# Two short down groups become one of four row blocks, and the plain last pair is finished token block by token block

## The chip, the core and the metric

The kernel runs on one core of a Trainium2 chip. The metric is the device time of one execution in microseconds. The core has a matrix engine (TensorE, PE in the profile; PEld is its loading of stationary operands), VectorE (DVE), ScalarE (ACT), GpSimd (POOL) and a queue for transfers (SyncE, SP). Matrix products are written to PSUM, which has eight banks; one bank holds 128 x 512 f32 values here. VectorE and ScalarE read the banks, and a bank can be written anew only when its reader is done.

## What is computed

One decoder layer over 512 tokens of width 1024. The part that the change touches is the feed-forward network (FFN), which stands at the beginning and near the end of the layer:

```python
def swiglu(x, w_gate, w_up, w_down):
    return (jax.nn.silu(x @ w_gate) * (x @ w_up)) @ w_down
...
    h = h + 0.5 * swiglu(rmsnorm(h, ffn1_norm[i]), ffn1_w_gate[i], ffn1_w_up[i], ffn1_w_down[i])
    n = rmsnorm(h, mix_norm[i]); z = n @ W_in          # attention and gated linear attention follow
    h = h + concat(attn_o, gla_o) @ w_out[i]
    h = h + 0.5 * swiglu(rmsnorm(h, ffn2_norm[i]), ffn2_w_gate[i], ffn2_w_up[i], ffn2_w_down[i])
    h = h + sigmoid(rmsnorm(h, ple_gate_norm[i]) @ ple_w_gate[i]) * emb
```

The inner width is 2816, that is 22 row blocks of 128. All of it is f32.

## The kernel before

Each f32 operand is held as the sum of two fp32r tiles, a rounded one (`hi`, made by ScalarE, line 130 for weights) and the remainder (`lo`, made by VectorE, line 131). A product of two operands is three matmuls into the same bank: hi x hi, hi x lo, lo x hi (`mm3`, line 172).

An FFN (`ffn`) walks over the 22 row blocks in 11 pairs; `fa` is the first block of a pair. For a pair it computes the gate projection (`gemm(0, ...)`, tiles `pg`, 48 matmuls of 512 columns) and the up projection (`gemm(1, ...)`, tiles `pu`, 48 matmuls), each in two banks of the tag `psT`. `factors` then applies silu, multiplies, and writes the result split in `acts_hi` and `acts_lo`. These have two slots, chosen by `j = (fa // 2) % 2`, so that two pairs are held at a time.

The down projection (`pd`) is not a plain product. `products(f0, f1)` takes a group of row blocks and uses seven products of sums and differences in the place of eight (a Strassen-Winograd scheme over halves of tokens, of columns and of even and odd row blocks). `ORDER` lists the products; for each the weights are one tile from the ring, and there are two token blocks `b`. A group of four row blocks needs 7 x 2 x 2 x 3 = 84 matmuls, one of two row blocks 42. Each product ends with two evictions by VectorE: into `U` (line 329, for products 1 and 6) or with `half_add` into the token tiles `h` (line 308, for the others). Products 2, 3 and 4 are added onto the banks of products 1, 5 and 7 after their first reading. Banks come from the tags `psA` (products 1 and 7) and `psG` (products 5 and 6), two banks each. At the end of an FFN `U` is added into three quarters of `h`, six instructions of line 308.

The last pair, row blocks 20 and 21, is multiplied plainly: for each column half `c0` and each of the four token blocks `t` six matmuls into a bank of `psA`, then a `half_add`. With the second column half a token block is complete and `done(t)` starts the next layer's normalization of it (two squares on ScalarE, a power on POOL, `nrm` on VectorE, line 261), and the transposes of block t - 1 (`ntr`, line 268, banks of `psG`), whose results are cast and subtracted once more. Behind the first FFN stands the mixing layer, which begins with `kvr`; behind the second the gate of the embeddings, `pgt`.

The groups before are (0, 4), (4, 8), (8, 12), (12, 16), (16, 18) and (18, 20). The first five run between gate and up projection of the pair that follows them; the sixth runs behind the loop, as does the plain pair:

```python
                if fa + 2 < NF and groups[0][1] == fa:
                    products(*groups.pop(0))
                gemm(1, 0, 512)
            factors(fa, pss)
        products(*groups.pop(0))
```

Weights come by transfers of SP's queue into raw tiles, are split, and lie in a ring of five `hi` and five `lo` tiles, with two more for the FFN's weights. `W.get(key)` splits up to four units ahead of the one that it is asked for, in the order in which `add_ffn` lists them. A ring tile comes free when its last matmul is done. A down group's weights are loaded as two transfers, even and odd row blocks.

The order of the instructions on each engine is laid down when the program is built: a scheduler takes them by program order as soon as their operands and banks are free in a timeline that it keeps (`schedule_with_timeline_sim=True`). So matmuls of the up projection fill places in which a product of the group isn't ready, and the queue of an engine isn't the order of the text.

Of the kernel before, what the change touches and what calls it, by code (L numbers as in the profile page):

```python
# [8 lines left out]
F32 = mybir.dt.float32  # L9
# [8 lines left out]
NT = S // P  # L18
# [3 lines left out]
NF = F // P  # L22
# [1 line left out]
NEG = -3.0e38  # L24
LEVELS = (64, 32, 16, 8, 4, 2, 1)

GROUPS = ((0, 4), (4, 8), (8, 12), (12, 16), (16, 18), (18, 20))

ORDER = ((1, 0), (5, 1), (2, 2), (3, 6), (7, 5), (6, 4), (4, 3))

# [110 lines left out]
def hymba_kernel(tc, A, out):  # L141
    nc = tc.nc
# [11 lines left out]
    def psA(name):  # L154
        return psp.tile([P, 512], F32, name=name, tag="psA", bufs=2)
# [16 lines left out]
    def mm3(o, l, r, start, stop_, **kw):  # L172

        mm(o, l[0], r[0], start, False, **kw)
        mm(o, l[0], r[1], False, False, **kw)
        mm(o, l[1], r[0], False, stop_, **kw)
# [14 lines left out]
    h = [hp.tile([P, D], F32, name=f"h{t}") for t in range(NT)]  # L191
    W = Weights(nc, rawp, ringp, 4)


    def add_ffn(i):
        g, u, d = A[f"ffn{i}_w_gate"], A[f"ffn{i}_w_up"], A[f"ffn{i}_w_down"]
        groups = [x for x in GROUPS]
        for f in range(0, NF, 2):
            W.add_cols(f"g{i}", g, f * P, 2)
            if f + 2 < NF and groups and groups[0][1] == f:  # L200
                W.add_products(f"d{i}", d, *groups.pop(0))
            W.add_cols(f"u{i}", u, f * P, 2)
        W.add_products(f"d{i}", d, *groups.pop(0))
        for c0 in (0, 512):
            W.add_rows(f"d{i}", d, NF - 2, 2, c0, 512)

# [71 lines left out]
    def tokens(t):  # L278
        return slice(t * P, (t + 1) * P)
# [10 lines left out]
    def ffn(i, nT, p, done, hi_p, raw_p, raw_tag, n_extra, rest=None):  # L290
        U = [p.tile([P, 512], F32, name=f"U{i}_{b}") for b in range(2)]
        acts_hi = hi_p.tile([P, 2, 7, 256], F32R, name=f"ahi{i}", tag="nlo")
# [14 lines left out]
        def half_add(hs, x):  # L307
            nc.vector.scalar_tensor_tensor(hs, x, 0.5, hs, ALU.mult, ALU.add)  # L308
# [29 lines left out]

        def factors(fa, pss):

            plain = fa == NF - 2
            j = (fa // 2) % 2
            cb = p.tile([P, 7, 256], F32, name=f"cb{i}_{fa}", tag="cb", bufs=1)
            for q in range(2):
                pg, pu = pss[q]
                sg = p.tile([P, S], F32, name=f"sg{i}_{fa + q}", tag="sg", bufs=2)
                nc.scalar.activation(sg, pg, AF.Silu)
                nc.vector.tensor_mul(cb[:, 2 * q:2 * q + 2, :].rearrange("p a c -> p (a c)"), pu, sg)  # L348
            n = 4 if plain else 7
            if not plain:  # L350
                nc.vector.tensor_sub(cb[:, 5, :], cb[:, 1, :], cb[:, 0, :])
                nc.vector.tensor_add(cb[:, 1, :], cb[:, 1, :], cb[:, 3, :])
                nc.vector.tensor_sub(cb[:, 4, :], cb[:, 1, :], cb[:, 0, :])
                nc.vector.tensor_sub(cb[:, 6, :], cb[:, 2, :], cb[:, 4, :])
            nc.scalar.copy(acts_hi[:, j, :n], cb[:, :n])
            nc.vector.tensor_sub(acts_lo[:, j, :n], cb[:, :n], acts_hi[:, j, :n].bitcast(F32))

        groups = list(GROUPS)
        for fa in range(0, NF, 2):
            pss = [(psT(f"pg{i}_{fa + q}"), psT(f"pu{i}_{fa + q}")) for q in range(2)]  # L360

            def gemm(m, a, b):
                for q in range(2):
                    wh, wl = W.get((f"{'gu'[m]}{i}", fa + q))
                    for k in range(KC):
                        mm3(pss[q][m][:, a:b], (wh[:, k, :], wl[:, k, :]),
                            (nT[0][:, k, a:b], nT[1][:, k, a:b]), k == 0, k == KC - 1)

            if fa == 0:
                gemm(0, 0, 256)  # L370
                gemm(1, 0, 256)
                if rest:
                    rest()
                gemm(0, 256, 512)
                gemm(1, 256, 512)
            else:
                gemm(0, 0, 512)
                if fa + 2 < NF and groups[0][1] == fa:
                    products(*groups.pop(0))
                gemm(1, 0, 512)  # L380
            factors(fa, pss)
        products(*groups.pop(0))
        for b in range(2):
            half_add(h[b][:, r], U[b])
            half_add(h[2 + b][:, l], U[b])
            half_add(h[2 + b][:, r], U[b])
        for c0 in (0, 512):
            wh, wl = W.get((f"d{i}", c0, NF - 2))
            for t in range(NT):
                ps = psA(f"pd{i}_{c0}_{t}")  # L390
                for q in range(2):
                    a = (1, 2 * q + t // 2, tokens(t % 2)) if ((NF - 2) // 2) % 2 else (0, 2 * q + t // 2, tokens(t % 2))
                    mm3(ps, tuple(x[:, a[0], a[1], a[2]] for x in (acts_hi, acts_lo)), (wh[:, q, :], wl[:, q, :]),
                        q == 0, q == 1)
                half_add(h[t][:, c0:c0 + 512], ps)
                if c0:
                    done(t)
        W.extra = None


# [590 lines left out]
```

## Time and profile before

| what | value |
|---|---|
| median of 3 runs | 1037.27 us (1036.75 to 1039.93) |
| the profiled execution's own time | 1041.27 us |
| its span, first to last instruction | 1039.5 us |
| mean granted TensorE clock | 0.986 |
| TensorE busy | 1006.9 us, 97% |
| VectorE busy | 673.4 us, 65% |
| ScalarE busy | 398.1 us, 38% |
| chain that ended last | 87% TensorE, 5% VectorE, 3% transfers |

The profile is of one execution. Matmuls are pipelined, and their ends are modelled, so that a busy TensorE isn't necessarily one at its peak: starts that follow each other are the better measure of its pace. The granted clock is a share of 2.4 GHz; 0.5 is the lower level, 1.2 GHz. A wait is put down to the semaphore that came last.

### The profile page before, as it was taken

What the parts mean: (1) busy time and instruction counts of PE and PEld (TensorE: products, weight loads), DVE (VectorE), ACT (ScalarE), POOL (GpSimd) and SP (SyncE); (2) the same over time, 40 slices, a digit from 0 to 9 for tenths busy, and PEclk for the clock granted to TensorE, in tenths of its full rate; (3) what the DMA queues carried; (4) which work ended last, traced back from release to release, by engine and by line L of the source; (5) the groups of instructions that cost most, each with busy time, mean ns of one, the idle gap of its engine ahead of it and who ended that gap; (6) DMA issues with size and microseconds to landing.
All of it is one profiled execution on the core that took longest, in us unless ns stands there. A gap on an engine that the chain in (4) does not pass through costs nothing.

```text
span 1039.5 us, 12500 instructions
## 1 busy us (share of the span) xinstructions
PE 1006.9 (97%) x5090; PEld 823.6 (79%) x5090; DVE 673.4 (65%) x904; ACT 398.1 (38%) x585; POOL 47.0 (5%) x58
## 2 busy tenths in 40 slices
PE   6999999999999979999999999999999999999798
PEld 5988888888888858877667789888888888887577
DVE  6486756666667586568875454767576666685853
ACT  6344333333323335554474243343323333233331
POOL 2300000000000001100000100000000000000100
PEclk9899999999999999999999799999999999999999
DMA  6843325042212053131103315242250523120521
GB/s 242 275 173 123 120 75 169 0 162 82 100 63 82 1 185 102 41 122 26 57 22 81 122 54 208 83 158 84 81 162 1 167 76 122 41 82 8 186 80 52
DMA packets 73148, 105.79 MB, mean 102 GB/s; under 512 B 5745, under 2 KB 55170, under 8 KB 73090
## 3 DMA queue, kind: packets, MB, share of 16 engines
q1 hardware_dynamic: 70786, 96.60, 28.4%
q0 software_dynamic: 2304, 8.39, 2.1%
q8 instruction: 40, 0.66, 0.3%
q14 instruction: 18, 0.15, 0.0%
HBM read 98.69 MB, written 6.29 MB: 101 GB/s over the span
## 4 chain that ended last, share of the span: by engine, by line
PE 87%; DVE 5%; DMA 3%; issue 2%; ACT 1%; POOL 1%; SPq 0%; ACTq 0%; POOLq 0%; DVEq 0%
PE pu L170 23%; PE pg L170 23%; PE pd L170 17%; PE pgt L170 4%; PE wo L170 3%; PE gv L170 2%; PE aq L170 2%; PE gqk L170 2%; DVE wlo L131 2%; PE gog L170 2%; DVE h L308 2%; PE gr L170 1%; PE sc L170 1%; PE pv L170 1%; PE kvr L170 1%
## 5 line engine op out<-in xcount | busy, mean ns | idle before, releaser
L130 ACT CAST whi<-wraw 128x1024 fp32r<-128x1024 f32 (+1 forms) x130 | 134.0, 1040 | 196.6 <-PE pd L170 123.6
L131 DVE TENSOR_TENSOR wlo<-wraw,whi 128x1024 fp32r<-128x1024 f32 (+1 forms) x126 | 151.5, 1206 | 59.5 <-ACT whi L130 56.6
L170 PE MATMUL pg<-nhi_f,whi 128*128 128x512 f32 (+1 forms) x384 | 143.2, 375 | 2.3 <-ACT nhi_f L241 2.3
L170 PE MATMUL pg<-nlo_f,whi 128*128 128x512 f32 (+1 forms) x384 | 144.0, 375 | 0.0
L170 PE MATMUL pg<-nhi_f,wlo 128*128 128x512 f32 (+1 forms) x384 | 143.2, 374 | 0.0
L170 PE MATMUL pu<-nhi_f,whi 128*128 128x512 f32 (+1 forms) x384 | 142.5, 372 | 0.5 <-DVE h L895 0.5
L170 PE MATMUL pu<-nlo_f,whi 128*128 128x512 f32 (+1 forms) x384 | 142.6, 372 | 0.0
L170 PE MATMUL pu<-nhi_f,wlo 128*128 128x512 f32 (+1 forms) x384 | 142.2, 371 | 0.0
L170 PE MATMUL pd<-whi,ahi 128*128 128x512 f32 x312 | 124.1, 398 | 12.5 <-DVE h L308 12.4
L170 PE MATMUL pd<-wlo,ahi 128*128 128x512 f32 x312 | 122.6, 393 | 0.0
L170 PE MATMUL pd<-whi,alo 128*128 128x512 f32 x312 | 122.3, 393 | 0.0
L308 DVE SCALAR_TENSOR_TENSOR h<-pd,h 128x512 f32<-128x512 f32 x136 | 90.1, 685 | 30.2 <-PE pd L170 29.9
L170 PEld LDWEIGHTS pg<-nhi_f,whi 128*128 128x128 f32 x384 | 72.9, 191 | 15.5 <-ACT nhi_f L241 3.0
L170 PEld LDWEIGHTS pg<-nlo_f,whi 128*128 128x128 f32 x384 | 73.4, 191 | 12.6 <-DVE nlo_f L242 0.2
L170 PEld LDWEIGHTS pd<-whi,ahi 128*128 128x128 f32 x312 | 59.2, 190 | 30.1 <-DVE h L308 9.6
L170 PEld LDWEIGHTS pg<-nhi_f,wlo 128*128 128x128 f32 x384 | 73.1, 191 | 12.4
L170 PEld LDWEIGHTS pu<-nhi_f,whi 128*128 128x128 f32 x384 | 72.3, 188 | 13.2 <-DVE h L895 0.7
L170 PEld LDWEIGHTS pu<-nlo_f,whi 128*128 128x128 f32 x384 | 72.3, 188 | 12.5
L130 ACT CAST whi<-draw 128x1024 fp32r<-128x1024 f32 (+1 forms) x42 | 38.0, 908 | 115.6 <-PE pu L170 56.2
L170 PEld LDWEIGHTS pu<-nhi_f,wlo 128*128 128x128 f32 x384 | 72.3, 188 | 12.4
L130 ACT CAST whi<-wpr 128x1024 fp32r<-128x1024 f32 (+1 forms) x42 | 38.1, 909 | 112.8 <-PE pu L170 60.8
L348 DVE TENSOR_TENSOR cb<-pu,sg 128x512 f32<-128x512 f32 x44 | 30.4, 690 | 77.2 <-PE pu L170 76.5
(242 smaller groups left out, 1530.7 us busy)
## 6 DMA issues: line engine op xcount, KB each, us to landing
wraw<-in_ffn_w_gate_dram SPq DMA_DIRECT2D x22, 1024.0 KB, 5.2
wraw<-in_ffn_w_up_dram SPq DMA_DIRECT2D x22, 1024.0 KB, 5.2
wpr<-in_ffn_w_down_dram SPq DMA_DIRECT2D x8, 1024.0 KB, 5.6
wraw<-in_w_in_dram SPq DMA_DIRECT2D x8, 1024.0 KB, 5.0
draw<-in_ffn_w_down_dram SPq DMA_DIRECT2D x8, 1024.0 KB, 5.2
wraw<-in_ple_w_gate_dram SPq DMA_DIRECT2D x4, 1024.0 KB, 5.1
h<-in_x_dram SPq DMA_DIRECT2D x4, 512.0 KB, 8.7
emb_d<-eo POOLq DMA_DIRECT2D x4, 512.0 KB, 10.4
```

The source lines that it names most:

```text
L130: nc.scalar.copy(hi, v)
L131: (nc.gpsimd if u in (2, 3) else nc.vector).tensor_tensor(lo, v, hi.bitcast(F32), op=ALU.subtract)
L170: nc.tensor.matmul(o, lhsT=l, rhs=r, start=start, stop=stop_, **kw)
L308: nc.vector.scalar_tensor_tensor(hs, x, 0.5, hs, ALU.mult, ALU.add)
L348: nc.vector.tensor_mul(cb[:, 2 * q:2 * q + 2, :].rearrange("p a c -> p (a c)"), pu, sg)
```

## The change

Both files differ in the down projection alone. The groups (16, 18) and (18, 20) become one group (16, 20), which runs between gate and up projection of the last pair (`fa` = 20), as the other groups do one pair after their last block. The six additions of `U` follow it there, before the last up projection. `factors` splits the last pair's activations in two halves, one for each row block, instead of in one instruction each. The plain products of the last pair run over token blocks first: blocks 0 and 1 together, then block 2, then block 3; each block's two column halves lie in a bank of `psA` and one of `psG`, and all of the row block 20 (`q = 0`) stands ahead of row block 21. When a set of blocks is summed, both halves are added into `h` and `done(t)` is called. The units of the weights are listed in the order of their use.

```diff
@@ -24,7 +24,7 @@
 NEG = -3.0e38
 LEVELS = (64, 32, 16, 8, 4, 2, 1)
 
-GROUPS = ((0, 4), (4, 8), (8, 12), (12, 16), (16, 18), (18, 20))
+GROUPS = ((0, 4), (4, 8), (8, 12), (12, 16), (16, 20))
 
 ORDER = ((1, 0), (5, 1), (2, 2), (3, 6), (7, 5), (6, 4), (4, 3))
 
@@ -194,13 +194,12 @@
 
     def add_ffn(i):
         g, u, d = A[f"ffn{i}_w_gate"], A[f"ffn{i}_w_up"], A[f"ffn{i}_w_down"]
-        groups = [x for x in GROUPS]
         for f in range(0, NF, 2):
             W.add_cols(f"g{i}", g, f * P, 2)
-            if f + 2 < NF and groups and groups[0][1] == f:
-                W.add_products(f"d{i}", d, *groups.pop(0))
+            for f0, f1 in GROUPS:
+                if f1 == f:
+                    W.add_products(f"d{i}", d, f0, f1)
             W.add_cols(f"u{i}", u, f * P, 2)
-        W.add_products(f"d{i}", d, *groups.pop(0))
         for c0 in (0, 512):
             W.add_rows(f"d{i}", d, NF - 2, 2, c0, 512)
 
@@ -338,24 +337,25 @@
 
         def factors(fa, pss):
 
-            plain = fa == NF - 2
             j = (fa // 2) % 2
             cb = p.tile([P, 7, 256], F32, name=f"cb{i}_{fa}", tag="cb", bufs=1)
             for q in range(2):
                 pg, pu = pss[q]
                 sg = p.tile([P, S], F32, name=f"sg{i}_{fa + q}", tag="sg", bufs=2)
                 nc.scalar.activation(sg, pg, AF.Silu)
-                nc.vector.tensor_mul(cb[:, 2 * q:2 * q + 2, :].rearrange("p a c -> p (a c)"), pu, sg)
-            n = 4 if plain else 7
-            if not plain:
+                half = slice(2 * q, 2 * q + 2)
+                nc.vector.tensor_mul(cb[:, half].rearrange("p a c -> p (a c)"), pu, sg)
+                if fa == NF - 2:
+                    nc.scalar.copy(acts_hi[:, j, half], cb[:, half])
+                    nc.vector.tensor_sub(acts_lo[:, j, half], cb[:, half], acts_hi[:, j, half].bitcast(F32))
+            if fa < NF - 2:
                 nc.vector.tensor_sub(cb[:, 5, :], cb[:, 1, :], cb[:, 0, :])
                 nc.vector.tensor_add(cb[:, 1, :], cb[:, 1, :], cb[:, 3, :])
                 nc.vector.tensor_sub(cb[:, 4, :], cb[:, 1, :], cb[:, 0, :])
                 nc.vector.tensor_sub(cb[:, 6, :], cb[:, 2, :], cb[:, 4, :])
-            nc.scalar.copy(acts_hi[:, j, :n], cb[:, :n])
-            nc.vector.tensor_sub(acts_lo[:, j, :n], cb[:, :n], acts_hi[:, j, :n].bitcast(F32))
-
-        groups = list(GROUPS)
+                nc.scalar.copy(acts_hi[:, j], cb)
+                nc.vector.tensor_sub(acts_lo[:, j], cb, acts_hi[:, j].bitcast(F32))
+
         for fa in range(0, NF, 2):
             pss = [(psT(f"pg{i}_{fa + q}"), psT(f"pu{i}_{fa + q}")) for q in range(2)]
 
@@ -375,26 +375,32 @@
                 gemm(1, 256, 512)
             else:
                 gemm(0, 0, 512)
-                if fa + 2 < NF and groups[0][1] == fa:
-                    products(*groups.pop(0))
+                for f0, f1 in GROUPS:
+                    if f1 == fa:
+                        products(f0, f1)
+                if fa == NF - 2:
+                    for b in range(2):
+                        half_add(h[b][:, r], U[b])
+                        half_add(h[2 + b][:, l], U[b])
+                        half_add(h[2 + b][:, r], U[b])
                 gemm(1, 0, 512)
             factors(fa, pss)
-        products(*groups.pop(0))
-        for b in range(2):
-            half_add(h[b][:, r], U[b])
-            half_add(h[2 + b][:, l], U[b])
-            half_add(h[2 + b][:, r], U[b])
-        for c0 in (0, 512):
-            wh, wl = W.get((f"d{i}", c0, NF - 2))
-            for t in range(NT):
-                ps = psA(f"pd{i}_{c0}_{t}")
-                for q in range(2):
-                    a = (1, 2 * q + t // 2, tokens(t % 2)) if ((NF - 2) // 2) % 2 else (0, 2 * q + t // 2, tokens(t % 2))
-                    mm3(ps, tuple(x[:, a[0], a[1], a[2]] for x in (acts_hi, acts_lo)), (wh[:, q, :], wl[:, q, :]),
-                        q == 0, q == 1)
-                half_add(h[t][:, c0:c0 + 512], ps)
-                if c0:
-                    done(t)
+        j = ((NF - 2) // 2) % 2
+        tiles = [W.get((f"d{i}", c0, NF - 2)) for c0 in (0, 512)]
+        for ts in ((0, 1), (2,), (3,)):
+            ps = {}
+            for q in range(2):
+                for t in ts:
+                    for c, bank in enumerate((psA, psG)):
+                        if q == 0:
+                            ps[t, c] = bank(f"pd{i}_{c}_{t}")
+                        wh, wl = tiles[c]
+                        mm3(ps[t, c], tuple(x[:, j, 2 * q + t // 2, tokens(t % 2)] for x in (acts_hi, acts_lo)),
+                            (wh[:, q, :], wl[:, q, :]), q == 0, q == 1)
+            for t in ts:
+                half_add(h[t][:, l], ps[t, 0])
+                half_add(h[t][:, r], ps[t, 1])
+                done(t)
         W.extra = None
```

## Rows read from the trace of the kernel before

**Rows 1.** The page's part 1: busy us, share of the span, instructions
```profile
PE 1006.9 (97%) x5090; PEld 823.6 (79%) x5090; DVE 673.4 (65%) x904; ACT 398.1 (38%) x585; POOL 47.0 (5%) x58
```

**Rows 2.** The chain that ended last: start us, us, what, around FFN 1's tail
```profile
336.40 10.88 PE pg L170 x48
347.28 10.89 PE pu L170 x48
359.48 1.20 DVE U L329 x2
```

**Rows 3.** Windows: busy us of each engine (instructions), granted clock (PEclk), DMA
```profile
212.64:242.56 29.92, 29.92 (x133) 24.77 (x133) 20.84 (x25) 9.99 (x11) 0.00 (x0) 1.00 0.52 174
275.20:305.12 29.92, 29.92 (x133) 24.77 (x133) 21.32 (x29) 8.22 (x11) 0.00 (x0) 1.00 0.36 124
316.00:336.40 20.40, 20.40 (x91) 16.89 (x91) 18.64 (x25) 7.93 (x9) 0.00 (x0) 1.00 0.28 89
357.99:386.98 28.99, 23.66 (x91) 17.34 (x89) 25.60 (x39) 9.80 (x17) 0.57 (x1) 0.94 0.44 140
386.98:390.80 3.82, 2.15 (x16) 1.57 (x15) 3.69 (x8) 2.94 (x9) 0.81 (x2) 1.00 0.77 302
560.00:592.00 32.00, 31.22 (x121) 23.60 (x121) 15.29 (x30) 7.80 (x16) 6.54 (x8) 0.79 0.33 108
953.16:984.18 31.02, 23.85 (x91) 17.18 (x89) 26.57 (x38) 10.42 (x16) 1.08 (x2) 0.94 0.37 124
984.18:987.38 3.20, 1.96 (x11) 1.16 (x11) 3.20 (x7) 2.96 (x7) 2.49 (x4) 1.00 0.96 356
372.90:376.30 3.40, 3.40 (x10) 2.65 (x8) 3.40 (x7) 0.00 (x0) 0.00 (x0) 0.51 0.76 263
973.80:976.90 3.10, 3.10 (x7) 2.45 (x8) 1.28 (x3) 0.72 (x2) 0.00 (x0) 0.50 0.67 259
```

**Rows 4.** Groups by line, TensorE, first tail: busy us, mean ns | idle, releaser
```profile
L170 PE MATMUL pd<-whi,ahi 128*128 128x512 f32 x30 | 13.0, 432 | 5.3 <-DVE h L308 5.3
```

**Rows 5.** The same of the second tail, 953.16 to 984.18
```profile
L170 PE MATMUL pd<-whi,ahi 128*128 128x512 f32 x30 | 13.2, 438 | 7.2 <-DVE h L308 7.1
```

**Rows 6.** Groups by line and form, VectorE, first tail, 357.99 to 386.98
```profile
L308 DVE SCALAR_TENSOR_TENSOR h<-pd,h 128x512 f32<-128x512 f32 x17 | 11.0, 682 | 1.8 <-PE pd L170 1.8
L308 DVE SCALAR_TENSOR_TENSOR h<-U,h 128x512 f32<-128x512 f32 x6 | 3.8, 682 | 0.0
...
L329 DVE TENSOR_TENSOR U<-U,pd 128x512 f32<-128x512 f32 x4 | 2.6, 679 | 0.0
```

**Rows 7.** Timeline of TensorE, first tail and what follows it
```profile
357.99 0.39 PE L170 MATMUL pd<-whi,ahi 128*128 128x512 f32 x1
...
372.08 0.47 PE L170 MATMUL pd<-whi,ahi 128*128 128x512 f32 x1 [1.86 <-DVE h L308]
...
386.75 0.39 PE L170 MATMUL pd<-whi,alo 128*128 128x512 f32 x1
387.19 1.07 PE L268 MATMUL ntr_mx<-idn,nrm_mx 128*128 128x128 f32 x8
```

**Rows 8.** Groups by line and form, whole span: 512-wide cast, subtraction and product
```profile
L348 DVE TENSOR_TENSOR cb<-pu,sg 128x512 f32<-128x512 f32 x44 | 30.4, 690 | 77.2 <-PE pu L170 76.5 <-ACT sg L347 0.7
...
L131 DVE TENSOR_TENSOR wlo<-wpr,whi 128x512 fp32r<-128x512 f32 x14 | 9.5, 687 | 7.3 <-ACT whi L130 7.3
...
L130 ACT CAST whi<-wpr 128x512 fp32r<-128x512 f32 x14 | 8.6, 622 | 34.5 <-PE pu L170 14.5 <-PE pd L170 9.3 <-PE pg L170 9.2
```

**Rows 9.** Timeline of VectorE: from a block's last sum to its normalized rows
```profile
383.38 1.28 DVE L308 SCALAR_TENSOR_TENSOR h<-pd,h 128x512 f32<-128x512 f32 x2
...
385.76 1.28 DVE L261 SCALAR_TENSOR_TENSOR nrm_mx<-h,rs_mx,gain_mix_norm 128x1024 f32<-128x1024 f32 x1 [0.75 <-POOL rs_mx L248]
```

**Rows 10.** Timeline of ScalarE and VectorE: a ring tile of the next layer, second tail
```profile
978.36 1.05 ACT L130 CAST whi<-wraw 128x1024 fp32r<-128x1024 f32 x1 [3.83 <-PE pd L170]
...
979.44 1.22 DVE L131 TENSOR_TENSOR wlo<-wraw,whi 128x1024 fp32r<-128x1024 f32 x1 [0.45 <-ACT whi L130]
```

## The prediction, made before the changed kernel was run

> **What bounds the kernel now.** I read the page's part 1 first: TensorE is busy for 97% of the span [rows 1]. That says only that a gain has to come out of TensorE's waits, or out of fewer matmuls. So the second view was the chain of work that ended last, in order of time. Inside an FFN it is TensorE alone: 48 matmuls of 512 columns take 10.88 us, so one costs 10.88 / 48 = 0.2267 us, and the chain leaves TensorE for VectorE only behind the last up projection [rows 2]. The third view, the windows, shows the same as two kinds of stretch. Where a down group shares its time with an up projection, TensorE does 84 + 48 = 132 matmuls in 29.92 us, which is 132 x 0.2267 us with nothing over; a group of two row blocks does 42 + 48 = 90 in 20.40 us, again with nothing over [rows 3]. Then come the two tails, 357.99 to 386.98 and 953.16 to 984.18: from the first matmul behind the last up projection to the end of the last down matmul [rows 3, 7]. Each holds 90 matmuls (42 of the product group (18, 20), 48 of the plain pair), worth 90 x 0.2267 = 20.40 us, and they take 28.99 and 31.02 us. So 8.59 and 10.62 us are lost, 19.21 together. The same windows say to whom: VectorE is busy for 25.60 of 28.99 and 26.57 of 31.02 us [rows 3]. The groups by line agree: TensorE's waits in a tail end with VectorE's `half_add` of line 308, which sets PSUM banks free (5.3 and 7.1 us) [rows 4, 5], one of them 1.86 us long [rows 7]. The rest of the loss is weight loads held up with them, and a drop of the clock: behind the longest waits the granted clock stands at 0.51 and 0.50, which is the 1.2 GHz level, for about 3 us in either tail [rows 3].
>
> **The change, part by part.** The number of matmuls does not change: before, 4 x 84 + 2 x 42 + 48 = 468 per FFN; after, 5 x 84 + 48 = 468. What changes is where they stand and what VectorE does beside them.
>
> (1) *The last groups.* The 42 matmuls that stood beside block 18's up projection and the 42 of the tail become one group of 84 between gate and up of blocks 20 and 21. That is the shape of the stretches at 212.64 and 275.20, which lose nothing [rows 3]. So 42 matmuls leave each tail and cost their bare 42 x 0.2267 = 9.52 us in a stretch that is bound by TensorE; those at block 18 move at the same price. Seven evictions of two banks, 14 instructions of 0.68 us [rows 6], disappear per FFN, since six groups become five; as VectorE does not bound the stretches where they go, I give nothing for that beyond the tail. Four weight loads of half size on SP's queue become two full ones per FFN, with the same bytes, and a whole gate projection (10.88 us) covers them.
>
> (2) *The six additions of U* move from the tail into the stretch of the last up projection. Six cost 3.8 us of VectorE [rows 6]. The stretch at 275.20 has VectorE at 21.32 of 29.92 us [rows 3]; with them 25.1. They are covered by 4.8 us of room; without that room they would cost at most their 3.8 us per FFN, and what would be late is the first half of the last pair's activations. Taken: 0.
>
> (3) *The last pair's factors, in halves.* Now the plain matmuls stand directly behind the last up matmul and need the activations of blocks 20 and 21. Block 20's are made while block 21's up projection runs (24 matmuls, 5.44 us). Block 21's chain starts with the last up matmul: product 0.69, cast 0.62, subtraction 0.69 us [rows 8], 2.0 us, some 2.2 with the starts. It is covered by the 12 matmuls of q = 0 for two token blocks, 12 x 0.2267 = 2.72 us. If VectorE is inside another instruction, say a subtraction of 1.22 us [rows 10], up to 1.2 us appear less the 0.5 to spare; behind that wait stand the whole rest of the tail and the next layer's transposes. Taken: 0.3 us per FFN, bounds 0 and 2.2.
>
> (4) *The plain tail.* 48 matmuls, 10.88 us, on four banks instead of two. Block 0's first sum is complete after 15 of them (3.4 us); with a `half_add` of 0.68 us its bank is free by about 4.4 us, and block 2 wants it after 24 matmuls (5.44 us). So no wait; VectorE has 8 of them, 5.4 us, in 10.88. Each wait of the tail that is gone also takes the clock's drop with it, which is inside the 8.59 and 10.62 us.
>
> (5) *The handover* to the next layer takes 3.82 and 3.20 us before its matmuls run densely [rows 3]: eight transposes [rows 7], then cast and subtraction. I leave both as they are. With a block's normalization ready sooner it may shrink by all but the transposes (about 1 us): -2.8 and -2.2. On the other side both plain weight tiles are now held to the end of the tail, where the first was free half-way; the next layer's tile that takes its place then comes a cast of 1.05 and a subtraction of 1.22 us later [rows 10]: at most +2.3 each.
>
> Sum: -8.59 - 10.62 + 2 x 0.3 = **-18.6 us**. The profiled execution took 1041.27 us for a span of 1039.5, so it should give 1022.7 with a span of 1020.9. The median of the three runs, 1037.27, is 4.0 below the profiled one; the same step gives 1037.27 - 18.6 = **1018.7 us**. Its own range is 1018.7 - 5.0 to 1018.7 + 4.6, or 1014 to 1023.
>
> **Rivals.**
> *Blocks and transposes queue for the same two banks* (0.11). The column half c = 1 takes its banks from `psG`, and so do the next layer's transposes. If the queue, laid down at build, sets block 0's transposes ahead of block 2's matmuls, TensorE waits for block 0's normalization. From the first of a pair of half additions to the end of the normalized rows go 387.04 - 383.38 = 3.7 us [rows 9]. Block 0 is summed after 18 matmuls (4.1 us), so its rows come at about 8; TensorE has been out of work since 5.44: 2.7 us, once or twice per FFN, 5.4 to 10.8 us in all, against which the handover gives back up to 5.0. Against it: in the trace all blocks' matmuls ran before the first transpose [rows 7]. Time: about 1024. The Trainium skill, Perfetto Trace Analysis, section Matmuls, asks that independent groups rotate through different PSUM banks; by that rule this sharing is the change's weak place, while the second bank pair of (4) follows it. No run here shows yet which weighs more.
>
> *The half clock* (0.03), the case that ends slower. In either tail the clock fell to the 1.2 GHz level [rows 3]. If the shorter waits of the new tail, one per block, let it fall early, each matmul costs about 0.2 us more. It decides from 18.6 / 0.2 = 93 matmuls at that level: nearly the 96 of both tails. If both tails and the first 24 matmuls of both next layers (whatever their width, at most 0.2 each) run so, the loss is 144 x 0.2 = 28.8 us and the time about 1047. Against it: the fall at 372.9 came behind a wait of 1.86 us [rows 7], and I expect none of 1 us. The Trainium skill, TensorE: Matmul & The Clock Gate, section A second HAM failure mode: psum-queue depth-cycling, tells of a kernel whose short idles between groups let the clock swing between its two levels; that would make this case likelier. The trace agrees only in that the clock falls inside a tail; outside the short stretches at 0.51 and 0.50 it held, since the tails' means are 0.94 [rows 3].
>
> *The loss only moves* (0.04). The group of 84 would have to starve in the last up stretch as it did in the tail. For that VectorE would need more than 29.92 us of work there; I count 25.1. Time 1037, no change.
>
> *A redrawn mixing layer* (0.08). The order on each engine is laid down anew at build, and the layer between the FFNs is not bound by TensorE throughout: from 560 to 592 the granted clock is 0.79, so 0.21 x 32 = 6.7 us are lost there [rows 3]. Another order may lose that once more: about 1025.
>
> **Chances and range.** The forecast has 0.74, and with the first and the last rival the kernel is faster: 0.93. A measurement of this kernel can tell about 0.3% from no change. Within that: 0.04. Slower: 0.03. The range goes from 1013 (handover hidden, nothing lost) to 1026 (the bank rival's middle, the redrawn layer); what it leaves out is the bank rival's upper part, the two cases at 1037 and 1047, and a small part of the forecast's own, together about 2 in 10.
>
> **What would show it.** Right: in each FFN the last up projection ends about 9.5 us later than before, the stretch of 132 matmuls before it stays at 29.92 us, 48 matmuls follow in 11 to 12 us with the clock at 1.00, and TensorE's waits for line 308 in the tail fall below 1 us. Wrong step by step: a window of the last up stretch over 31 us (steps 1, 2); a wait on the activations over 1 us (step 3); transposes between the plain blocks with a wait ahead of them (bank rival); granted clock of the tail under 0.9 (clock); a mixing layer longer than before (last rival).

## The result and the profile after

The changed kernel takes 1023.25 us (median of 4 runs, 1022.14 to 1024.25); the kernel before, run beside it, takes 1038.6 (median of 4). The ratio is 0.9851, with a 95% interval of 0.9825 to 0.9877: 15.4 us faster, where 18.6 had been forecast. The time lies 4.6 us above the forecast of 1018.7; 3.2 of them are missing gain, and the other 1.3 are the kernel before, which took 1038.6 here and not 1037.27. The profiled execution took 1024.25 us, with a span of 1022.4 (1020.9 was forecast for it) and a mean granted clock of 0.995.

The page's part 1 of the changed kernel, to be read against [rows 1]:

```profile
PE 998.1 (98%) x5090; PEld 820.4 (80%) x5090; DVE 657.0 (64%) x856; ACT 397.4 (39%) x573; POOL 47.8 (5%) x58
```

The number of matmuls is the same, 5090; VectorE has 48 instructions less. The windows of the changed kernel (columns as in [rows 3]) show where the time came from and where it stayed:

```profile
337.88:367.64 29.76, 29.76 (x134) 24.63 (x132) 21.80 (x30) 8.16 (x10) 0.00 (x0) 1.00 0.30 91
923.80:953.56 29.76, 29.76 (x133) 24.62 (x132) 22.23 (x29) 8.31 (x9) 0.00 (x0) 1.00 0.37 124
367.64:373.10 5.46, 5.46 (x25) 4.32 (x23) 2.52 (x4) 1.27 (x2) 0.00 (x0) 1.00 0.51 164
373.10:381.37 8.27, 4.74 (x23) 3.33 (x22) 7.68 (x13) 5.30 (x13) 1.96 (x2) 1.00 0.37 145
381.37:385.20 3.83, 3.83 (x13) 3.27 (x14) 1.24 (x2) 0.24 (x1) 0.00 (x0) 0.55 0.00 0
953.56:959.20 5.64, 5.60 (x25) 4.32 (x23) 3.20 (x5) 1.58 (x2) 0.00 (x0) 1.00 0.00 0
967.27:971.90 4.63, 4.63 (x14) 3.63 (x15) 1.79 (x4) 1.33 (x4) 0.98 (x2) 0.64 0.44 169
560.00:592.00 32.00, 31.32 (x148) 24.74 (x147) 16.76 (x31) 9.44 (x17) 6.54 (x8) 1.00 0.33 116
366.00:400.00 34.00, 29.70 (x172) 25.46 (x171) 19.39 (x31) 13.26 (x31) 4.00 (x6) 0.95 0.29 107
950.00:1000.00 50.00, 46.72 (x211) 37.45 (x210) 29.98 (x41) 20.03 (x36) 5.47 (x8) 0.97 0.23 80
```

The two stretches of the last up projection (first two lines) are full: TensorE is busy for the whole 29.76 us of the windows, with VectorE at 21.80 and 22.23. The first 24 plain matmuls follow without a gap (5.46 of 5.46 us, and 5.60 of 5.64). Then, from 373.10 to 381.37, TensorE is busy for 4.74 of 8.27 us, and in the next stretch its granted clock is 0.55 on average. The second tail has the same pattern, with 0.64 from 967.27 on. The timeline of TensorE in both tails names the wait:

```profile
375.97 0.39 PE L170 MATMUL pd<-whi,alo 128*128 128x512 f32 x1
377.33 1.06 PE L267 MATMUL ntr_mx<-idn,nrm_mx 128*128 128x128 f32 x8 [0.97 <-DVE nrm_mx L260]
378.63 0.40 PE L170 MATMUL kvr<-whi,nhi_mix 128*128 128x272 f32 x1 [0.24 <-ACT nhi_mix L240]
378.87 0.29 PE L170 MATMUL kvr<-wlo,nhi_mix 128*128 128x272 f32 x1
381.37 0.69 PE L170 MATMUL pd<-whi,ahi 128*128 128x512 f32 x1 [2.22 <-DVE nlo_mix L241]
...
388.55 0.50 PE L170 MATMUL pd<-whi,ahi 128*128 128x512 f32 x1
...
963.23 1.06 PE L267 MATMUL ntr_pg<-idn,nrm_pg 128*128 128x128 f32 x8 [0.93 <-DVE nrm_pg L260]
...
967.27 0.50 PE L170 MATMUL pd<-whi,ahi 128*128 128x512 f32 x1 [2.01 <-DVE nlo_pg L241]
```

The matmul of 375.97 is the last of the first column half of blocks 2 and 3 (12 matmuls from 373.35 on, banks of `psA`). What stands next on TensorE is not the second half of block 2 but the eight transposes of block 0, then two matmuls of `kvr`, and only at 381.37 block 2's second half, 2.22 us late; block 3's follows at 388.55, behind the transposes of block 1. VectorE's timeline in the first tail shows what held it:

```profile
375.90 1.28 DVE L260 SCALAR_TENSOR_TENSOR nrm_mx<-h,rs_mx,gain_mix_norm 128x1024 f32<-128x1024 f32 x1 [0.15 <-POOL rs_mx L247]
...
377.77 1.22 DVE L131 TENSOR_TENSOR wlo<-wraw,whi 128x1024 fp32r<-128x1024 f32 x1
379.43 1.28 DVE L260 SCALAR_TENSOR_TENSOR nrm_mx<-h,rs_mx,gain_mix_norm 128x1024 f32<-128x1024 f32 x1 [0.44 <-POOL rs_mx L247]
380.63 1.28 DVE L241 TENSOR_TENSOR nlo_mix<-ntr_mx,nhi_mix 128x512 fp32r<-128x512 f32 x2
```

Block 0's rows are normalized at 375.90 to 377.18 and transposed at once, but their subtraction (`nlo_mix`, 380.63, which sets the `psG` banks free) stands behind a weight subtraction (377.77) and the normalization of block 1, which itself waits 0.44 us for POOL's power. Block 2's matmuls of 381.37 need these banks. That is the rival of the blocks and transposes that queue for the same two banks, in both tails. The order can be read in the program: `done(1)` asks for the transposes of block 0, with two banks of `psG`, before the loop comes to block 2 and asks for its bank of `psG`; `done(2)` does the same with block 1 ahead of block 3. TensorE takes them in this order in both tails.

### The profile page after: what moved, and what is told of

It is laid out like the page before. It is cut to its first block, busy times and chain, and to the rows that moved or that the text cites. A ratio compares the mean times of both kernels' runs of the same rounds, so it can differ in the third digit from the quotient of the medians.

```text
span 1022.4 us, 12395 instructions
## 1 busy us (share of the span) xinstructions
PE 998.1 (98%) x5090; PEld 820.4 (80%) x5090; DVE 657.0 (64%) x856; ACT 397.4 (39%) x573; POOL 47.8 (5%) x58
## 4 chain that ended last, share of the span: by engine, by line
PE 93%; DVE 3%; DMA 1%; ACT 1%; POOL 1%; issue 0%; POOLq 0%
PE pu L170 23%; PE pg L170 23%; PE pd L170 20%; PE pgt L170 4%; PE wo L170 4%; PE gog L170 2%; PE gv L170 2%; PE aq L170 2%; PE gqk L170 2%; PE gr L170 2%; PE sc L170 1%; PE pv L170 1%; PE o L170 1%; PE pe L170 1%; DMA wraw<-in_ffn_w_gate_dram 1%; DVE h L307 1%
## 5 line engine op out<-in xcount | busy, mean ns | idle before, releaser
L170 PE MATMUL pd<-whi,alo 128*128 128x512 f32 x312 | 120.0, 391 | 0.0
L307 DVE SCALAR_TENSOR_TENSOR h<-pd,h 128x512 f32<-128x512 f32 x116 | 76.8, 686 | 37.2 <-PE pd L170 37.2
L170 PEld LDWEIGHTS pg<-nhi_f,whi 128*128 128x128 f32 x384 | 72.8, 190 | 15.4 <-ACT nhi_f L240 3.0
L130 ACT CAST whi<-draw 128x1024 fp32r<-128x1024 f32 x35 | 36.8, 1054 | 99.0 <-PE pu L170 54.7
L130 ACT CAST whi<-wpr 128x1024 fp32r<-128x1024 f32 x35 | 36.9, 1055 | 98.6 <-PE pu L170 59.0
```

Source lines behind the costliest of these rows:

```text
L130: nc.scalar.copy(hi, v)
L170: nc.tensor.matmul(o, lhsT=l, rhs=r, start=start, stop=stop_, **kw)
```

## The experiments

To compare stretches, three landmarks are used, which stand in the chain of every profile: the start of the first dense gate projection (10.91 us, 48 matmuls), the start of the mixing layer's last dense run of `wo` (102 matmuls), and the start of the second FFN's first dense gate projection. "First part" is from the first to the second, "second part" from the third to the end of the span; between second and third lie 57.5 us in all of them. The table holds the median and the ratio of all runs, and the parts of the one profiled execution.

| kernel | median us (runs) | ratio to before, 95% | first part | second part |
|---|---|---|---|---|
| before, first profile | 1037.27 (3) | | 537.60 | 389.49 |
| before, run again | 1037.74 (10) | 0.9979 [0.9958, 1.0001] | 533.26 | 390.61 |
| the change | 1023.25 (4) | 0.9851 [0.9825, 0.9877] | 528.38 | 381.51 |
| second half on `psT` | 1027.49 (4) | 0.9888 [0.9859, 0.9917] | 525.40 | 384.30 |
| groups only | 1022.5 (4) | 0.9842 [0.9818, 0.9867] | 524.95 | 381.46 |
| blocks only | 1036.23 (10) | 0.9976 [0.9953, 1.0] | 534.76 | 386.20 |
| transposes on `psT` | 1018.68 (4) | 0.9810 [0.9784, 0.9836] | 526.95 | 377.65 |
| U late | 1025.11 (4) | 0.9884 [0.984, 0.9927] | 528.93 | 379.79 |
| whole factors | 1028.41 (8) | 0.9911 [0.9885, 0.9938] | 529.63 | 380.86 |
| groups, two tags | 1027.08 (4) | 0.9893 [0.9875, 0.9912] | 527.86 | 383.16 |
| groups, transposes on `psT` | 1020.7 (6) | 0.9827 [0.9803, 0.985] | 530.22 | 379.84 |
| transposes on `psT`, again | 1015.86 (5) | 0.9784 [0.9759, 0.9809] | 522.50 | 377.73 |
| the change, again | 1022.86 (4) | 0.9845 [0.9824, 0.9866] | 528.17 | 379.90 |

### The kernel before, run again

No edit. The mixing layer of the first profile of before had a granted clock of 0.79 from 560 to 592 us [rows 3], and the changed kernel's profile has 1.00 there (the line of 560.00 in its windows). Was that the change's doing?

> The kernel before, unchanged, profiled once more. In the profiles of before and after the mixing layer has the same order of instructions on TensorE, yet it took 5.9 us more before, where the granted clock stood at 0.50 from about 572 to 584 us. Theory A (that fall of the clock is an accident of one execution): a second profile shows that stretch at 1.00 in some execution, with a span some 4 to 6 us shorter, 1034 to 1036. Theory B (the old tail brings it about through the times that it leaves behind): the fall is there again at the same place and the span is again 1039 to 1040.

The first part took 533.26 us instead of 537.60, and the same window of the same kernel reads:

```profile
560.00:592.00 32.00, 31.33 (x154) 24.58 (x153) 18.57 (x33) 12.48 (x24) 6.53 (x8) 1.00 0.50 150
```

So this fall belongs to one execution and not to the kernel, as theory A had it; the first part is 4.3 us shorter without it. The span is 1038.2 all the same, and not the 1034 to 1036 of the theory: the second part is 1.1 us longer, and the start up to the first landmark 1.9. Profile against profile, the change is compared with this second one.

### The second column half on other banks

```diff
-                    for c, bank in enumerate((psA, psG)):
+                    for c, bank in enumerate((psA, psT)):
```

> The kernel after, with the second column half of the plain blocks in banks of psT in place of psG, so that they share none with the transposes. Bank theory (blocks 2 and 3 wait for a bank that block 0's and block 1's transposes hold): TensorE's waits of 2.2 and 2.0 us in the tails and the drop of the clock behind them go; of the 7.4 and 6.3 us that the tails with the handover lose after the change, some 5 and 4 come back: 1013 to 1016 us. Rival (the wait is for VectorE and the normalization, whichever bank is used): 1021 to 1025 us as after.

The time is 1027.49, about 4 us above that of the change (the intervals of the two ratios just overlap) and outside both expected ranges. In the profiles the first part is 3.0 us shorter and the second 2.8 longer. The tag `psT` has four banks where `psG` has two, so that the second halves of all four blocks have a bank at once and none waits for another's; matmuls of blocks 2 and 3 now stand ahead of the sums of block 0. The second tail, first TensorE's timeline, then VectorE's, then a window:

```profile
968.21 1.94 PE L267 MATMUL ntr_pg<-idn,nrm_pg 128*128 128x128 f32 x8 [4.79 <-DVE ms_pg L258]
```

```profile
959.59 4.28 DVE L307 SCALAR_TENSOR_TENSOR h<-pd,h 128x512 f32<-128x512 f32 x7 [4.30 <-PE pd L170]
963.78 1.22 DVE L131 TENSOR_TENSOR wlo<-wraw,whi 128x1024 fp32r<-128x1024 f32 x1
964.91 0.15 DVE L258 SCALAR_TENSOR_TENSOR ms_pg<-ss_pg 128x1 f32<-128x1 f32 x1
```

```profile
968.00:972.00 4.00, 3.34 (x12) 2.43 (x13) 3.63 (x6) 2.40 (x6) 0.99 (x2) 0.50 1.00 381
```

VectorE waits 4.30 us for the first sum, then does seven half additions in a row (4.28 us) and a weight subtraction (1.22 us) before it takes up block 0's mean square at 964.91. TensorE has run out of plain matmuls by then; it waits 4.79 us for the first transposes (2.24 us in the first tail), and behind the wait its granted clock is 0.50, the 1.2 GHz level. The bank wait is gone and a wait for the normalization stands in its place.

### The groups alone, and the blocks alone

"Groups only" is the changed kernel with the plain pair in its old order, "blocks only" the kernel before with the plain pair in its new order:

```diff
-        for ts in ((0, 1), (2,), (3,)):
...
+        for c0 in (0, 512):
+            wh, wl = W.get((f"d{i}", c0, NF - 2))
+            for t in range(NT):
+                ps = psA(f"pd{i}_{c0}_{t}")
```

> The kernel after, but with the plain pair in the old order: column half by column half, all blocks in turn, psA alone. Theory (moving the 42 matmuls out of the tail brings the whole gain, the new order of the blocks gives some of it back): 1017 to 1021 us, 2 to 6 us faster than the whole change. Rival (finishing blocks in turn is what brings it): 1028 us or more.

> The kernel before, with its six groups, and only the plain pair in the new order, over psA and psG. Theory: the tail still holds 42 matmuls of the last group and VectorE's evictions of them, and the shared banks add waits: 1036 to 1044 us, no gain. Rival (the new order brings the gain by itself): 1030 us or less.

Groups only: 1022.5 us, no different from the change within the intervals. That is between the theory's 1017 to 1021 and the rival's 1028: the new order brings no gain here, but gives none back either. Blocks only: 1036.23, as the theory had it, with a ratio whose interval reaches to 1. So the gain of 15 us is that of the groups and of what goes with them (the place of the additions of U, the halves of the factors). The waits of the first tail with the groups only, from TensorE's timeline:

```profile
371.31 0.50 PE L170 MATMUL pd<-whi,ahi 128*128 128x512 f32 x1 [0.55 <-DVE h L307]
...
377.37 0.50 PE L170 MATMUL pd<-whi,ahi 128*128 128x512 f32 x1 [0.33 <-DVE h L307]
...
381.75 0.39 PE L170 MATMUL kvr<-whi,nhi_mix 128*128 128x272 f32 x1 [0.24 <-ACT nhi_mix L240]
...
383.63 0.66 PE L267 MATMUL ntr_mx<-idn,nrm_mx 128*128 128x128 f32 x4 [1.36 <-DVE nlo_mix L241]
```

Four waits of 0.55, 0.33, 0.24 and 1.36 us, 2.5 together, and the granted clock is 1.00 throughout this tail. With the last group out of the tail, two banks cost the plain pair 0.9 us.

### The transposes on other banks

The transposes that follow the two tails take `psT`; the plain blocks keep `psA` and `psG`:

```diff
-                norm_transpose(*pend[t - 1])
+                norm_transpose(*pend[t - 1], psT)
```

and in the same way at the three other places behind the tails.

> The kernel after, with the next layer's transposes in banks of psT; the plain blocks keep psA and psG and their order. Theory (the blocks and the transposes shared psG, and that alone held blocks 2 and 3 back; the order of the blocks is good when they have banks of their own): no wait between the plain matmuls, block 0's normalized rows are there when block 3 is done, 1012 to 1016 us. Rival (what the run with the second half on psT showed: with the banks apart, TensorE waits for block 0's normalization anyway, 2 to 5 us per FFN): 1020 to 1027 us.

1018.68 us, between the theory's 1016 and the rival's 1020. In its profile the granted clock fell in the mixing layer, so it was run once more, beside the change on one chip:

> The changed kernel with the transposes on psT once more, beside the unchanged version of the change. Theory: the waits of 2.2 and 2.0 us and the half clock behind them came from the bank pair that plain blocks and transposes shared; without it the plain tails run densely, and the time is 4 to 6 us under that of the change: median 1017 to 1019, ratio to before 0.979 to 0.983. In its first profile the granted clock fell in the mixing layer (0.50 from 568 to 572 us), as it did in that of before; if that is chance, a profile without it has a span near 1016 us. Rival: the four times seen of it were low by luck, and it is within 2 us of the change, 1021 to 1023.

> The change, unaltered, on the same chip. Theory: as before, 1022 to 1024.5 with a wait of about 2 us ahead of block 2's second column half in both tails; the mixing layer near 176.7 us unless the clock falls there again. Rival: its lead over the kernel before depends on the chip or the execution, and it is outside 1020 to 1026.

1015.86 against 1022.86 us: 7.0 us on one chip, and the fastest version found; the theory had 1017 to 1019 for it, and the unaltered change came out as expected. All nine times of this kernel have a median of 1016.5, all eight of the change 1022.9, so 6.4 us. The timeline of TensorE in its first tail (the last line is of the mixing layer, for the end of this document):

```profile
367.78 0.39 PE L170 MATMUL pd<-whi,ahi 128*128 128x512 f32 x1
...
379.08 2.14 PE L267 MATMUL ntr_mx<-idn,nrm_mx 128*128 128x128 f32 x16
...
381.74 0.39 PE L170 MATMUL kvr<-whi,nhi_mix 128*128 128x272 f32 x1 [0.26 <-ACT nhi_mix L240]
...
382.47 0.39 PE L170 MATMUL kvr<-whi,nlo_mix 128*128 128x272 f32 x1 [0.22 <-DVE nlo_mix L241]
...
563.03 0.50 PE L170 MATMUL wo<-whi,nhi_mo 128*128 128x512 f32 x1 [0.67 <-ACT nhi_mo L240]
```

Windows of it, the first for the end of this document, the others to be read against the last two of the changed kernel:

```profile
560.00:592.00 32.00, 31.33 (x147) 25.15 (x147) 15.57 (x25) 8.63 (x14) 5.14 (x7) 1.00 0.39 132
366.00:400.00 34.00, 33.38 (x205) 29.27 (x204) 23.43 (x37) 16.92 (x36) 3.39 (x7) 1.00 0.37 132
950.00:1000.00 50.00, 48.95 (x228) 39.62 (x227) 29.93 (x43) 19.05 (x36) 5.15 (x8) 1.00 0.25 89
```

All 48 plain matmuls run from 367.78 to 379.08, 11.3 us for a bare 10.88; then come 16 transposes in a row and two waits of a quarter of a microsecond. TensorE is busy for 33.38 of 34 us where the change has 29.70, and for 48.95 of 50 where it has 46.72, at a granted clock of 1.00 instead of 0.95 and 0.97.

### The old order with its transposes on other banks

The edits of "groups only" and of "transposes on `psT`" together.

> Five groups, the plain pair in its old order (column half by column half, on the two banks of psA), and the transposes behind the two tails on psT instead of psG. Theory: with the old order psG has no part in the plain tail, so what the other banks can save is only the waits for the transposes' own banks, 1.36 us at the first handover and 0.64 us at the second; the waits of the plain blocks for psA (0.55 and 0.33 us in each tail) stay. Time about 2 us under that of the old order with the transposes on psG, 1020 to 1021. Rival: banks that come free earlier bring the transposes forward, before the rows are ready, as later blocks came forward where the second half had psT to itself; then TensorE waits for a normalization and the time is 1024 or more.

1020.7 us, inside the theory's range (the wait at the first handover is 0.77 us instead of 1.36); the 1.8 us that it lies under "groups only" are within the intervals. It is 4.8 above the new order with the same banks on the same chip. So the new order of the plain pair is worth some 5 us where the transposes have banks of their own, and nothing that could be seen where they share `psG`. (The first part of its profile, 530.22, holds a fall of the clock in the mixing layer.)

### The old order on two tags

"Groups only" with `ps = (psA, psT)[c0 // 512](...)`: four banks for the old order.

> The kernel with the groups alone changed (plain pair column half by column half), with the second half in banks of psT in place of psA. Theory (in that order the only waits between plain matmuls are 0.3 to 0.6 us for the two banks of psA, twice per FFN): 1 to 2 us less than with psA alone, 1020 to 1022 us. Rival (the free banks let the second half be multiplied early, so that all blocks are summed late and the normalization starts late, as with the blocks' second half on psT): 1025 us or more.

1027.08 us, slower than two banks by 4.6 (other chip; 0.9893 against 0.9842). TensorE's timeline, first and second tail, then VectorE's of the first:

```profile
383.77 1.94 PE L267 MATMUL ntr_mx<-idn,nrm_mx 128*128 128x128 f32 x8 [3.73 <-DVE ms_mx L258]
...
970.25 1.94 PE L267 MATMUL ntr_pg<-idn,nrm_pg 128*128 128x128 f32 x8 [4.78 <-DVE ms_pg L258]
```

```profile
376.00 4.28 DVE L307 SCALAR_TENSOR_TENSOR h<-pd,h 128x512 f32<-128x512 f32 x7 [4.73 <-PE pd L170]
```

As in the first try with `psT`, and as the rival had it: the later matmuls go early, the first sums come late (VectorE's first half addition starts 7.0 us after the first plain matmul, with the groups only 3.1), and TensorE waits 3.73 and 4.78 us for the first block's mean square.

### U late

The six additions of U stand behind the loop, as before:

```diff
-                if fa == NF - 2:
-                    for b in range(2):
-                        half_add(h[b][:, r], U[b])
...
+        for b in range(2):
+            half_add(h[b][:, r], U[b])
```

> The kernel after, with the six additions of U behind the loop in place of ahead of the last up projection. Theory of the prediction (VectorE has room in the last up stretch, so that moving them there takes work off the tail): here 3.7 us of VectorE's work come back into each tail, and some of it delays block 0's half additions: 1023 to 1030 us. Rival (VectorE idles in the new tail as well, so that it makes no difference where they stand): within 1.5 us of the kernel after, 1022 to 1025 us.

1025.11 us; the intervals of the two ratios overlap, and the profiled spans, one of each, are 1022.5 and 1022.4. But the run doesn't test the place of the additions, because the edit moved them in the text alone. VectorE's timeline of the change, then of this kernel, each with the first addition of U and the first sums of the plain blocks:

```profile
356.77 1.29 DVE L307 SCALAR_TENSOR_TENSOR h<-U,h 128x512 f32<-128x512 f32 x2
...
372.60 2.48 DVE L307 SCALAR_TENSOR_TENSOR h<-pd,h 128x512 f32<-128x512 f32 x4 [2.69 <-PE pd L170]
```

```profile
358.04 1.29 DVE L307 SCALAR_TENSOR_TENSOR h<-U,h 128x512 f32<-128x512 f32 x2
...
373.86 2.48 DVE L307 SCALAR_TENSOR_TENSOR h<-pd,h 128x512 f32<-128x512 f32 x4 [2.69 <-PE pd L170]
```

The additions stand in the same places of the last up stretch, and TensorE, VectorE, ScalarE and POOL work in the same order from end to end. That fits a scheduler that takes an instruction as soon as its operands are there. So this is the change run a third time, and its four times, 1022.31 to 1032.97 us, show how far one and the same order can scatter.

### Whole factors

The last pair's cast and subtraction are one instruction each again, over both row blocks:

```diff
-                if fa == NF - 2:
-                    nc.scalar.copy(acts_hi[:, j, half], cb[:, half])
...
+            if fa == NF - 2:
+                nc.scalar.copy(acts_hi[:, j, :4], cb[:, :4])
```

> The kernel after, with the last pair's activations cast and subtracted in one instruction each (1.05 and 1.22 us) behind the last up matmul, in place of two halves. Theory of the prediction (the halves hide the chain behind the first 12 plain matmuls): without them TensorE waits 2 to 3 us per FFN ahead of the plain part, 1027 to 1030 us. Rival (the wait for block 0's normalization later in the tail takes it up): within 1.5 us of the kernel after.

1028.41 us, inside the theory's range and 5 above the change; 3.3 above 1025.11, the same order as the change on this run's chip, where the intervals of the ratios overlap. TensorE's timeline in both tails shows the price at the place that the prediction named:

```profile
371.55 0.50 PE L170 MATMUL pd<-whi,ahi 128*128 128x512 f32 x1 [1.86 <-ACT ahi L349]
...
958.72 0.50 PE L170 MATMUL pd<-whi,ahi 128*128 128x512 f32 x1 [1.86 <-ACT ahi L349]
```

Two waits of 1.86 us for the activations, directly behind the last up matmul. The division into halves takes them away whole; the change itself shows none. Behind them the waits for block 2's bank are shorter, 1.44 and 1.23 us instead of 2.22 and 2.01, so that of the 3.7 us about 2.4 are left in the spans (1024.9 against 1022.4 and 1022.5).

## Why the prediction was right, and where it was wrong

The sign, the range of 1013 to 1026 and the mechanism of the gain held; the forecast was 4.6 us too low, just outside the 1014 to 1023 given as its own. One step was wrong, the plain tail, and two terms were too small, so that errors of opposite sign met.

*Step 1, the last groups: right.* The first matmul behind the last up projection starts at 367.64, 9.65 us later than the 357.99 of [rows 7], where 9.5 was written; in the second FFN, counted from its first dense gate projection, it is 9.52 us later. The chain of the changed kernel there:

```profile
337.88 8.16 PE pd L170 x36
...
361.00 6.80 PE pu L170 x30
367.80 4.77 PE pd L170 x21
...
372.60 2.48 DVE h L307 x4
```

TensorE alone up to 372.57, with no VectorE between up and down. In the chain the stretch of 132 matmuls runs from 337.88 to 367.80, 29.92 us as before [rows 3]. The loss of 8.59 and 10.62 us by way of line 308 is gone: of the waits for the half additions none above 0.6 us is left in the kernel with the groups only.

*Step 2, U: borne out by the room, its price not tested.* VectorE has 7.5 us of room or more in the stretch that took the additions (21.80 and 22.23 us where 25.1 was counted). What they would cost in the tail no run shows.

*Step 3, the halves: right, and cheaper than taken.* 0.3 us per FFN was taken; the first 24 plain matmuls lose 0 and 0.04. Undivided, it is 1.86 us per FFN in the trace and 3 to 5 us in the time.

*Step 4, the plain tail: wrong.* "So no wait" counted only the blocks and their half additions against the four banks. The banks of the second half had a third user, the transposes, and the program asks for theirs first. The 48 matmuls, forecast to follow in 11 to 12 us, end at 390.04, 22.4 us after the first, with the next layer's work between them. Block 0's first sum also came later than the 3.4 us counted: the first half addition starts 4.96 us after the first plain matmul (372.60), but that alone made no wait. The waits come to 0.97 + 0.24 + 2.22 = 3.4 us in the first tail and 0.93 + 0.24 + 2.01 = 3.2 us in the second. The clock behind them costs 0.45 x 3.83 = 1.7 and 0.36 x 4.63 = 1.7 us. Together 10.0 us in this profile, inside the 5.4 to 10.8 of the rival *Blocks and transposes queue for the same two banks*. That its size fits is in part luck: it priced the wait for block 0's rows at 2.7 us, which came to 0.97 because the first halves of blocks 2 and 3 ran meanwhile, and it left out the clock and the longest wait, 2.22 us for the eviction of the transposes. The rival had been given 0.11 because in the trace of before all blocks ran ahead of the first transpose [rows 7]; but there the plain pair did not use `psG` at all, so that row couldn't speak on this. Its time, 1024, is 0.75 us from the measured one.

The run with the transposes elsewhere puts the price at 7.0 us in the medians. In the parts of the profiles it is 528.17 - 522.50 = 5.7 and 379.90 - 377.73 = 2.2, or 7.8. It is less than 10.0 because the kernel without the shared banks has short waits at the handover too, and because in the second profile of the change the clock fell in the first tail only.

The Trainium skill, Perfetto Trace Analysis, section Matmuls, asks for independent groups of matmuls to rotate through different banks. The runs agree for the transposes (1022.86 to 1015.86 us). They also show that more banks are not enough by themselves: two versions that gave the second column half the four banks of `psT` became slower than those that shared (1027.49 against 1023.25, and 1027.08 against 1022.5), as the freed matmuls delayed the block that was wanted first.

*Step 5, the handover: too low.* It was left as it was, with -2.8 and -2.2 as the lower bounds. With the bank wait out of the way the kernel takes 1015.86 us, 2.8 under the forecast. Against the second profile of before its parts are shorter by 533.26 - 522.50 = 10.8 and 390.61 - 377.73 = 12.9, together 23.6 us. In that profile the 90 matmuls of the tails take 30.70 and 32.12 us, so they lose 10.30 and 11.72, which is 22.0 where the first profile had 19.2; the 48 of the kernel with its transposes on `psT` take 11.30 and 11.28 us, and lose 0.42 and 0.40. The tails thus give 21.2 us, and about 2.4 are left for the handover, half of its bound. So the sum was too small by the handover, put at 0, and by a loss in the tails read from one execution; the bank, some 7 us, went the other way. That the forecast missed by no more than 4.6 us is luck to that extent.

*The half clock* didn't decide, but it took part: in the first profile of the change a stretch of about 4 us in either tail, as in the kernel before. The same waits don't bring it down each time. The order of the change was profiled three times (the change, U late, the change again). At the wait of 2.22 us in the first tail the clock fell in all three; at that of 2.0 us in the second it fell in the first profile alone. From the change again, TensorE's timeline and a window of the second tail:

```profile
967.58 0.50 PE L170 MATMUL pd<-whi,ahi 128*128 128x512 f32 x1 [2.01 <-DVE nlo_pg L241]
```

```profile
950.00:1000.00 50.00, 46.74 (x218) 37.70 (x217) 30.21 (x42) 20.32 (x37) 5.47 (x8) 1.00 0.25 88
```

So of the two times 1.7 us above, the second belongs to one execution. The Trainium skill, TensorE: Matmul & The Clock Gate, section A second HAM failure mode: psum-queue depth-cycling, tells of a clock that swings between its levels through short idles. In the change it fell once per tail at most; the first tail of the blocks-only kernel agrees with it, with two falls (granted clock 0.54 from 378 to 382 us, 0.98 from 385 to 388, 0.57 from 388 to 392) at waits of 2.73 and 1.53 us. The shorter waits of the groups-only kernel, 0.55 and 0.33 us, left its tail at 1.00.

*A redrawn mixing layer* was wrong as a mechanism: what had looked like a loss by the order was an accident of the clock in one execution.

Why the second halves ran ahead of block 0's sums with `psT`, but not with `psG` when the transposes are elsewhere, can be read from the number of banks: `psT` has four, one for each block, while with the two of `psG` block 2's second half has to wait until block 0's bank has been read. Two banks of their own, and no more, is what the fastest version gives the second half. A version with four banks and matmuls held in the order of the blocks was not run.

## What to carry to other kernels

When a change gives work a bank, list every user of that bank's tag until it comes free again, those of the next stage included, and ask in which order the program asks for it; a trace in which the work didn't use the tag can't answer that. A second test belongs to it: which block is wanted first, and do more banks let later work pass it. Where a scheduler lays down the order, look in the trace whether an edit moved what it was to move before reading its time. Separate what one profile shows by accident, such as a clock that fell in one execution, from what the kernel does, before a term of the sum is taken from it.

## What the runs showed of the hardware

The granted clock can fall at a wait well under a microsecond, in one execution and not in another. Both profiles of the kernel with its transposes on `psT` have a wait of 0.68 or 0.67 us ahead of the same matmul of `wo`. Timeline and windows of the first (those of the second stand above, at the run of it again):

```profile
564.99 0.80 PE L170 MATMUL wo<-whi,nhi_mo 128*128 128x512 f32 x1 [0.68 <-ACT nhi_mo L240]
```

```profile
564.00:568.00 4.00, 3.33 (x11) 2.23 (x9) 2.05 (x4) 1.15 (x3) 0.80 (x1) 0.60 0.00 0
568.00:572.00 4.00, 4.00 (x12) 2.87 (x12) 0.76 (x2) 0.65 (x2) 0.21 (x1) 0.50 0.02 4
```

In the first the clock stands at 0.60 and 0.50 behind it (0.50 is the 1.2 GHz level), in the second it holds at 1.00 throughout. In both TensorE was busy without a gap of note in the 15 us before the wait. What decides between them no run here shows. The first parts are 526.95 and 522.50 us, 4.5 apart. The four times of the first run lie accordingly in two pairs, 1021.01 and 1020.71, 1016.5 and 1016.65, with mean granted clocks of 0.991 and 0.996 to 0.997. Such an accident is as large as the step that the forecast missed, so several executions of each kernel are needed to see a step of that size.
